# First and last weight matmul of every chunk carry one order mark: TensorE takes the 189 chunks whole, one behind the other

## Chip, cores and metric

One core of one Trainium2 chip runs the kernel. The metric is the device time of one execution in microseconds; lower is better. Every time in the text comes from the runs and the profiled execution of the kernel before.

## What is computed

Two transformer blocks, one behind the other, on a sequence of 256 positions with model width 1024, everything in float32. The first block has differential attention and block attention side by side; the second has two layers, each with retention, stick-breaking attention and a feed-forward part of width 4096.

```python
def first_block(x, p, ...):                       # DEPTH = 1
    h = rms_norm(x, norm_g[i])
    dq, dk, dv, dg, mq, mk, mv, mg, gates = split_in_proj(h @ w_in[i])
    y_a = (diff_attention(dq, dk, dv, ...) * silu(dg)) @ w_branch_diff[i]
    y_b = (moba_attention(mq, mk, mv) * silu(mg)) @ w_branch_moba[i]
    merged = sigmoid(g_a) * y_a + sigmoid(g_b) * y_b
    x = x + merged @ w_out[i]
    x = x + sigmoid(x @ w_ple_gate[i]) * (p[i] @ w_ple[i])
    return rms_norm(x, final_g)

def second_block(x, ...):
    for l in range(2):
        h = rmsnorm(x, g_mix[l])
        q_r, k_r, v_r, g_r, q_s, k_s, v_s, gate_a, gate_b = split(h @ w_in[l])
        ret = head_group_norm(retention(rotary(q_r), rotary(k_r), v_r)) * silu(g_r)
        sb = stick_breaking(q_s, k_s, v_s)
        merged = sigmoid(gate_a) * (ret @ p_ret[l]) + sigmoid(gate_b) * (sb @ p_sb[l])
        x = x + merged @ w_out[l]
        x = x + square(relu(rmsnorm(x, g_mlp[l]) @ w_up[l])) @ w_down[l]
    return rmsnorm(x, g_final)
```

## The kernel before

All weights come from DRAM as a stream of 189 chunks of 1 MB (`raw`, issued on SP's queue). This text numbers them C0 to C188 in stream order. Each chunk is split in two halves: ACT copies `raw` to a rounded high part `wh` (`split`, L294), DVE subtracts to get the low part `wl` (L295). The activations exist as the same kind of pair: `X2` is the normed input of a projection, hi by ACT (`norm_hilo`, L200) and lo by DVE (L201); `A2`, `B2` and `M2` are other such pairs (the names of the trace drop the digit). TensorE (PE) makes a product of full precision from three partial ones: `wh` against hi and lo together (one matmul of 512 columns) and `wl` against hi (256 columns), through the helper `mm` (L135).

The chunks that matter here: C0 to C36 are the first block (C20 is one of the four chunks `branch1` that multiply the attention's output `A2`; C33 to C36 are `w_ple_gate`). C37 to C112 are layer 0 of the second block: C37 is the first chunk of `w_in`, C38 and C39 the next ones; C66 is the first chunk of `p_sb`, which multiplies the stick-breaking output `B2`, eight heads that `sb_head` makes one after the other; C67 and C68 are gate chunks on `X2`; C77 to C80 are `w_out`, C81 to C88 the first of `w_up`. C113 to C188 are layer 1, where C142, C143, C144, C153 and C157 are what C66, C67, C68, C77 and C81 are in layer 0.

For a chunk with `fresh` set (C37, C77, C81, C113, C153, C157), `mm_t` first writes the partial products of the first six 128-row tiles of the input, and those of the last two tiles behind them, since the input is made tile by tile.

Of the attention, the last steps of a stick-breaking head are: `t` is exponentiated on ACT (L116), PE transposes it (L805, three matmuls), ACT and DVE split the result into `ph` and `pl` (L129, L130), PE multiplies it by the values (`mm3`, L138 to L140), and ACT and DVE split that into one tile of `B2`.

The order of the program is not the order of the source. The kernel is written with a tile framework whose scheduler simulates the engines and picks the next instruction of each engine among those that are free. An order token (`stamp_issue_order_token`) ties instructions with the same name to source order among themselves. Before the change the token "maps" stands on the last `mm` of the chunks i < LAST1 = 20 and on the score matmuls of the first block's attention heads (`soft_head`, L506). PE, ACT, DVE and POOL then execute their own queues in the order fixed by the scheduler, and wait on semaphores.

The main loop, at the end of `tile_blocks`, goes over the chunks: it issues the split of chunk i + 2 and the fetch of chunk i + 5, then runs `ch.banks(ch)` (the matmuls and what empties their banks), and lets each attention thread take one step.

Of the kernel before, what the change touches and what calls it, by code (L numbers as in the profile page):

```python
# [38 lines left out]
C_DEC = 1088  # L39
C_ALL = C_DEC + 4 * 384  # L40
NCHUNK = 189
LAST1 = 20


def _tables():
# [33 lines left out]
def tile_blocks(ctx: ExitStack, tc: tile.TileContext, a: dict, out: bass.AP):  # L79
    nc = tc.nc  # L80
    V, A, G, T = nc.vector, nc.scalar, nc.gpsimd, nc.tensor
# [21 lines left out]
    def acc():  # L103
        uid[0] += 1
        return psp.tile([P, 512], F32, tag="acc", bufs=NACC, name=f"acc_{uid[0]}")
# [23 lines left out]
        A.activation(hi, src, AF.Copy)  # L129
        V.tensor_sub(lo, src, f32(hi))  # L130

    last = [None]

    def mm(*args, **kw):
        last[0] = T.matmul(*args, **kw)  # L135

    def mm3(o, lh, ll, rh, rl, start, stop):
        T.matmul(o, lhsT=lh, rhs=rh, start=start, stop=False, skip_group_check=True)  # L138
        T.matmul(o, lhsT=lh, rhs=rl, start=False, stop=False, skip_group_check=True)  # L139
        T.matmul(o, lhsT=ll, rhs=rh, start=False, stop=stop, skip_group_check=True)  # L140


    xg = tl([GW + KT * S], "X")
# [33 lines left out]
    def use_consts():  # L177
        V.tensor_mul(gfm, g_fin, g_mix[0])
        V.tensor_scalar_mul(subg, subg, 1.0 - LAM_INIT)
        V.tensor_mul(lamv[:, 0:3:2], lamv[:, 0:3:2], lamv[:, 1:4:2])  # L180
        V.tensor_reduce(lam[:, 0:2], lamv[:, 0:3:2], AX.X, ALU.add)
        act(lam[:, 0:2], lam[:, 0:2], AF.Exp)
        V.tensor_sub(lam[:, 2:3], lam[:, 1:2], lam[:, 0:1])
        V.tensor_scalar_add(lam[:, 2:3], lam[:, 2:3], -LAM_INIT)
# [96 lines left out]
    def fetch(ch, n=1):  # L281

        ch.raw = shaped(ch, tl([2048], "raw", bufs=3))
        src = shaped(ch, a["wstream"][chunks.index(ch)])
        for k in pieces(ch, n):
            load(ch.raw[:, k], src[:, k])
            yield

    def split(ch, n=2):

        ch.wh = shaped(ch, tl([2048], "wh", F32R, bufs=3))
        ch.wl = shaped(ch, tl([2048], "wl", F32R, bufs=3))
        for k in pieces(ch, n):
            h = A.activation(ch.wh[:, k], ch.raw[:, k], AF.Copy)  # L294
            l = V.tensor_sub(ch.wl[:, k], ch.raw[:, k], f32(ch.wh[:, k]))  # L295
            yield h, l

    def mm_t(ch, ks, xs, j0, evac, n=2):
# [7 lines left out]
        def run(j, part, kinds):  # L306
            for m, i in ((m, i) for m in kinds for i in part):
                k, x = ks[i], xs[i]
                kw = dict(start=i == part[0] == 0 and m == kinds[0], stop=i == len(ks) - 1 and m == kinds[1],
                          skip_group_check=True)  # L310
                if m == 0:
                    mm(ps[j], lhsT=ch.wh[:, k, w[j]], rhs=x.rearrange("p c t -> p (c t)"), **kw)
                else:
                    mm(ps[j][:, 0:S], lhsT=ch.wl[:, k, w[j]], rhs=x[:, 0], **kw)
# [15 lines left out]
    def mm_2(ch, ks, xs, j0=0, n=2):  # L330

        ps = acc().rearrange("p (j t) -> p j t", j=2)
        for i, (k, x) in enumerate(zip(ks, xs)):
            for j in range(2):
                w = slice((j0 + j) * P, (j0 + j + 1) * P)
                mm3(ps[:, j], ch.wh[:, k, w], ch.wl[:, k, w], x[:, 0], x[:, 1], i == 0 and j == 0, i == len(ks) - 1)
        return ps

    def fold(ps, out=None):
# [6 lines left out]
    def mm_k(ch, ps, x, k0):  # L346

        for i in range(4):
            k = k0 + i
            for h in range(2):  # L350
                t = slice(h * P, (h + 1) * P)
                for n, (xs, ws) in enumerate(((x.h, ch.wh), (x.h, ch.wl), (x.l, ch.wh))):
                    mm(ps[h][0], lhsT=xs[:, k, t], rhs=ws[:, i], start=n == 0 and k == 0,
                       stop=n == 2 and k == KT - 1, skip_group_check=True)
# [26 lines left out]
    def chunk_2(w, c, x, evac, k0=0):  # L381
        def go(ch):
            ps = mm_2(ch, range(KT), [x().t[:, k] for k in range(KT)])
            run_pre()
            evac(ps, c)
        chunks.append(Chunk([wcols(w, c, k0)], go))
# [110 lines left out]
    def soft_head(idx, j, v, diff, wait):  # L497
# [42 lines left out]
        if diff:  # L540
            po = aux()[:, 0:S].rearrange("p (h e) -> p h e", h=2)
            h, l = wh[:, 0], wl[:, 0]
            vc = slice(j * P, (j + 1) * P)
            for i, (o, qt, kt) in enumerate(BLK):
                mm3(po[:, qt], h[:, o:o + P], l[:, o:o + P], vh[:, kt, vc], vl[:, kt, vc], i == 0, qt == kt)
            o = o_slot[idx % 2]
            ss = tl([2], "ss", bufs=2)
            for h in range(2):
                A.activation(o[:, h], po[:, h], AF.Square, accum_out=ss[:, h:h + 1])
            V.tensor_scalar(ss, ss, 1.0 / 128, EPS5, ALU.mult, ALU.add)  # L550
            G.tensor_tensor(ss, ss, mhalf[:, 0:2], ALU.pow)
            for h in range(2):
                A.activation(o[:, h], po[:, h], AF.Copy, scale=ss[:, h:h + 1])
            yield
            yield
            pt = aux()[:, 0:S]
            for h in range(2):
                T.transpose(pt[:, h * P:(h + 1) * P], o[:, h], ident)
            V.scalar_tensor_tensor(f, pt, subg, g1[:, idx], ALU.mult, ALU.mult)
        else:  # L560
            po = aux().rearrange("p (m q) -> p m q", m=2)
            vc = slice(j * P, (j + 1) * P)
            mm3(po, vh[:, 0, vc], vl[:, 0, vc], wh[:, :, 0:256], wl[:, :, 0:256], True, False)
            mm3(po[:, :, 128:256], vh[:, 1, vc], vl[:, 1, vc], wh[:, :, 256:384], wl[:, :, 256:384], False, True)
            for m in range(2):
                r = slice(m * 64, m * 64 + 64)
                V.tensor_mul(f[r], po[r, m], g1[r, idx])
# [78 lines left out]
    def branch1(c):  # L646
        def go(ch):
            if c == 0:
                start_merge()
            xs = [a1.t[:, k] for k in range(8)]  # L650
            ga, gb = sig(gates1, c, 0), sig(gates1, c, 1)
            pa, pb = mm_2(ch, range(4), xs[0:4]), mm_2(ch, range(4, 8), xs[4:8])
            V.tensor_mul(ga, ga, pa)
            V.tensor_mul(gb, gb, pb)
            G.tensor_add(ga, ga, gb)
            k = slice(2 * c, 2 * c + 2)
            hilo(mg.x.h[:, k], mg.x.l[:, k], ga)
            if c == 1:
                threads.append(ple_in())
        chunks.append(Chunk([wcols(("w_branch_diff", 0), c, 0, 4), wcols(("w_branch_moba", 0), c, 0, 4)], go))  # L660
# [21 lines left out]
    def ple(ch):  # L682
        for b in range(4):
            ps = mm_2(ch, range(2), [pt_.x.t[:, k] for k in range(2)], 2 * b)
            A.activation(pw[:, 2 * b:2 * b + 2], ps, AF.Copy)
# [352 lines left out]
    def drain(g):  # L1038
        for _ in g:
            pass  # L1040

    warm_up(WARM)
    f = fetch(chunks[0], 4)
# [7 lines left out]
    f = fetch(chunks[1], 2)  # L1051
# [5 lines left out]
    for i in range(2):  # L1057
        f = split(chunks[i], 4)
# [10 lines left out]
    for i, ch in enumerate(chunks):  # L1069
        if i + 2 < n:  # L1070
            drain(split(chunks[i + 2]))
        if i + 5 < n:
            drain(fetch(chunks[i + 5]))
        ready = list(threads)
        ch.banks(ch)
        if i < LAST1:
            tc.stamp_issue_order_token(last[0].ins, "maps")
        if i == 0:
            use_consts()
        for g in ready:  # L1080
            try:
                next(g)
            except StopIteration:
                threads.remove(g)
# [63 lines left out]
```

## Time and profile before

| what | value |
|---|---|
| median of 3 runs | 1146.5 us (1146.41 to 1147.41) |
| profiled execution | 1146.68 us, of which the span of the trace is 1144.8 us |
| PE busy | 1133.1 us, 6563 matmuls |
| DVE, ACT, POOL busy | 899.4, 708.4, 225.5 us |
| granted clock of TensorE, mean | 0.999 |

A busy share is an average over the span. PE has work nearly all the time, so the time is read from what PE does and from the few places where it waits. In the timeline a row gives the start of a run of like instructions and the time until the last of them ends; the next row may start before that, because matmuls overlap.

### The profile page before, as it was taken

Reading aid. Unit: us, or ns where it says so; the run is one execution under the profiler, and the core shown is the slowest. Engines: PE = TensorE matmul, PEld = TensorE weight load, DVE = VectorE, ACT = ScalarE, POOL = GpSimd, SP = SyncE. Lnnn points to the kernel's source line nnn. Section 1 sums busy time; section 2 is a strip of 40 time slices with the busy share of each in tenths; the row PEclk is TensorE's granted clock in tenths of the full one; section 3 lists DMA queues with packets and bytes.
Section 4 is the critical chain, followed back from the end, with each engine's and each line's share of the span. In section 5 each row is a group of like instructions: output and inputs, shape, how many; then the busy total and the mean of one; then the engine's idle time right before and its main releaser. Section 6 shows DMA issues by size and latency. Waiting matters only on the chain.

```text
span 1144.8 us, 17360 instructions
## 1 busy us (share of the span) xinstructions
PE 1133.1 (99%) x6563; PEld 994.1 (87%) x6563; DVE 899.4 (79%) x1487; ACT 708.4 (62%) x1286; POOL 225.5 (20%) x236
## 2 busy tenths in 40 slices
PE   9999999999999999999999999999999999999997
PEld 6888899998888888888888888888898888888887
DVE  6877787689988987788877778988886868967664
ACT  7788955476657665656654545556776656846542
POOL 0021231036442123220000014641121312000001
PEclk9999999999999999999999999999999999999999
DMA  8643455546544454545555556554444554555551
GB/s 319 230 162 132 148 184 185 184 175 206 195 175 163 147 182 149 204 181 202 185 184 187 197 188 210 182 191 163 182 148 147 201 193 177 207 198 184 185 184 38
DMA packets 32884, 207.63 MB, mean 181 GB/s; under 512 B 3873, under 2 KB 6433, under 8 KB 8737
## 3 DMA queue, kind: packets, MB, share of 16 engines
q1 hardware_dynamic: 32800, 206.52, 50.1%
q8 instruction: 52, 0.85, 0.3%
q14 instruction: 32, 0.25, 0.1%
HBM read 203.36 MB, written 1.05 MB: 179 GB/s over the span
## 4 chain that ended last, share of the span: by engine, by line
PE 93%; DVE 2%; DMA 1%; ACT 1%; issue 1%; POOL 1%; SPq 0%; POOLq 0%; DVEq 0%; ACTq 0%
PE acc L135 83%; PE acc L140 2%; PE acc L139 2%; PE acc L138 2%; PE aux L140 1%; PE aux L139 1%; PE aux L138 1%; DMA sig<-in_lambdas_dram 1%; PE aux L506 1%; DMA X<-in_xt_dram 1%; DVE wl L295 1%; PE aux L805 0%; ACT wh L294 0%; PE aux L489 0%; PE aux L535 0%
## 5 line engine op out<-in xcount | busy, mean ns | idle before, releaser
L295 DVE TENSOR_TENSOR wl<-raw,wh 128x1024 fp32r<-128x1024 f32 (+1 forms) x382 | 481.6, 1292 | 74.7 <-ACT wh L294 72.0
L294 ACT ACTIVATE wh<-raw 128x1024 fp32r<-128x1024 f32 (+1 forms) x382 | 380.8, 1044 | 144.3 <-PE acc L135 115.6
L135 PE MATMUL acc<-X,wh 128*128 128x512 f32 x1472 | 368.0, 393 | 0.3 <-DVE X L201 0.3
L135 PEld LDWEIGHTS acc<-X,wh 128*128 128x128 f32 x1472 | 266.8, 188 | 50.4 <-DVE X L201 0.5
L135 PE MATMUL acc<-X,wl 128*128 128x256 f32 x1472 | 202.3, 283 | 0.8 <-DVE f L343 0.8
L135 PEld LDWEIGHTS acc<-X,wl 128*128 128x128 f32 x1472 | 193.8, 191 | 9.6 <-DVE f L343 1.1
L342 ACT ACTIVATE f<-acc 128x256 f32<-128x256 f32 x216 | 80.1, 379 | 103.1 <-PE acc L135 102.2
L343 DVE TENSOR_TENSOR f<-f,acc 128x256 f32<-128x256 f32 x216 | 87.9, 415 | 67.8 <-ACT f L342 67.6
L135 PE MATMUL acc<-wh,X 128*128 128x512 f32 x448 | 119.0, 394 | 0.2
L135 PEld LDWEIGHTS acc<-wh,X 128*128 128x128 f32 x448 | 83.4, 188 | 18.3 <-ACT wh L294 1.5
L212 POOL TENSOR_TENSOR sq<-sq,f 128x256 f32<-128x256 f32 x24 | 26.5, 1102 | 263.6 <-ACT f L210 263.4
L624 POOL TENSOR_TENSOR sig<-f,nr 128x256 f32<-128x256 f32 x48 | 46.5, 976 | 119.9 <-DVE f L343 90.1
L693 DVE TENSOR_TENSOR X<-X,acc 128x256 f32<-128x256 f32 x112 | 45.9, 417 | 28.9 <-PE acc L135 27.8
L135 PE MATMUL acc<-wl,X 128*128 128x512 f32 x224 | 64.3, 394 | 0.0
L135 PE MATMUL acc<-B,wh 128*128 128x512 f32 x256 | 63.6, 391 | 0.0
L135 PE MATMUL acc<-A,wh 128*128 128x512 f32 x256 | 62.7, 391 | 0.0
L135 PEld LDWEIGHTS acc<-A,wh 128*128 128x128 f32 x256 | 47.0, 188 | 9.1
L135 PEld LDWEIGHTS acc<-B,wh 128*128 128x128 f32 x256 | 47.0, 188 | 9.0
L135 PEld LDWEIGHTS acc<-wl,X 128*128 128x128 f32 x224 | 41.7, 188 | 9.7 <-DVE wl L295 1.5
L135 PE MATMUL acc<-M,wh 128*128 128x512 f32 x192 | 48.0, 392 | 0.0
L573 POOL TENSOR_TENSOR G<-f,nr 128x256 f32<-128x256 f32 x24 | 21.5, 894 | 94.8 <-DVE f L343 94.7
L135 PEld LDWEIGHTS acc<-M,wh 128*128 128x128 f32 x192 | 34.6, 188 | 6.3
(229 smaller groups left out, 1623.4 us busy)
## 6 DMA issues: line engine op xcount, KB each, us to landing
raw<-in_wstream_dram SPq DMA_DIRECT2D x187, 1024.0 KB, 4.8
sig<-f SPq DMA_DIRECT2D x32, 64.0 KB, 4.4
B<-in_tables_dram SPq DMA_DIRECT2D x2, 768.0 KB, 5.9
raw<-in_wstream_dram SPq DMA_DIRECT2D x4, 256.0 KB, 4.4
raw<-in_wstream_dram SPq DMA_DIRECT2D x2, 512.0 KB, 7.4
M<-in_xn_dram SPq DMA_DIRECT2D x1, 1024.0 KB, 11.4
out_dram<-M SPq DMA_DIRECT2D x4, 256.0 KB, 2.2
X<-in_xt_dram SPq DMA_DIRECT2D x3, 256.0 KB, 6.1
```

The lines of the kernel that those rows point to most:

```text
L135: last[0] = T.matmul(*args, **kw)
L138: T.matmul(o, lhsT=lh, rhs=rh, start=start, stop=False, skip_group_check=True)
L139: T.matmul(o, lhsT=lh, rhs=rl, start=False, stop=False, skip_group_check=True)
L140: T.matmul(o, lhsT=ll, rhs=rh, start=False, stop=stop, skip_group_check=True)
L212: (V if k == KT - 1 else G).tensor_add(sq, sq, t)
L294: h = A.activation(ch.wh[:, k], ch.raw[:, k], AF.Copy)
L295: l = V.tensor_sub(ch.wl[:, k], ch.raw[:, k], f32(ch.wh[:, k]))
L342: A.activation(t, ps[:, S:2 * S], AF.Copy)
L343: V.tensor_add(t, t, ps[:, 0:S])
L573: G.tensor_mul(dst()[:, k], fold(ps), st.n.rb)
L624: G.tensor_mul(store[(c, i)][0][:, k % 2], fold(ps), st.n.rb)
L693: V.tensor_add(X[:, k], X[:, k], ps[:, o:o + S])
```

## The change

`mm` now collects every weight matmul of a chunk in `ends`, the projections made by `mm_2` (`mm3`) too. After `ch.banks(ch)` the first and the last of them get the token "maps", in all 189 chunks. No instruction is added or removed: both programs have 6563 matmuls. The line numbers of the changed kernel are 4 higher from the norm helpers on (L135 becomes L134, L138 to L140 become L142 to L144, L805 becomes L809).

```diff
-LAST1 = 20
...
-    last = [None]
+    ends = []
 
     def mm(*args, **kw):
-        last[0] = T.matmul(*args, **kw)
...
+        ends.append(T.matmul(*args, **kw))
+
+    def in_one(ends):
+
+        for ins in ends:
+            tc.stamp_issue_order_token(ins.ins, "maps")
+
+    def mm3(o, lh, ll, rh, rl, start, stop, f=T.matmul):
+        f(o, lhsT=lh, rhs=rh, start=start, stop=False, skip_group_check=True)
+        f(o, lhsT=lh, rhs=rl, start=False, stop=False, skip_group_check=True)
+        f(o, lhsT=ll, rhs=rh, start=False, stop=stop, skip_group_check=True)
...
-                mm3(ps[:, j], ch.wh[:, k, w], ch.wl[:, k, w], x[:, 0], x[:, 1], i == 0 and j == 0, i == len(ks) - 1)
+                mm3(ps[:, j], ch.wh[:, k, w], ch.wl[:, k, w], x[:, 0], x[:, 1], i == 0 and j == 0, i == len(ks) - 1, mm)
...
+        del ends[:]
         ch.banks(ch)
-        if i < LAST1:
-            tc.stamp_issue_order_token(last[0].ins, "maps")
+        in_one((ends[0], ends[-1]))
```

On PE the order changes at some fifteen places; written as rows of like instructions, PE's program has 2062 rows before and 1838 after. The two largest places follow.

PE at the start of layer 0, before: `wh_381` and `wl_382` are the weights of C37, `wh_390` and `wl_391` of C38, `wh_399` and `wl_400` of C39.

```order
L135 MATMUL acc_402_2680<-X2_366_2422,wh_381_2518 128x512 x2
L135 MATMUL acc_403_2693<-X2_366_2422,wl_382_2519 128x256 x3
L135 MATMUL acc_428_2790<-X2_366_2422,wh_390_2595 128x512 x2
L135 MATMUL acc_431_2818<-X2_366_2422,wl_391_2596 128x256
L135 MATMUL acc_403_2693<-X2_366_2422,wl_382_2519 128x256
L135 MATMUL acc_431_2818<-X2_366_2422,wl_391_2596 128x256 x3
L135 MATMUL acc_402_2680<-X2_366_2422,wh_381_2518 128x512
L135 MATMUL acc_428_2790<-X2_366_2422,wh_390_2595 128x512
L135 MATMUL acc_402_2680<-X2_366_2422,wh_381_2518 128x512
L135 MATMUL acc_428_2790<-X2_366_2422,wh_390_2595 128x512
L135 MATMUL acc_437_2854<-wh_399_2672,X2_366_2422 128x512 x4
L135 MATMUL acc_437_2854<-wl_400_2673,X2_366_2422 128x512 x4
```

The same place on PE after the change:

```order
L134 MATMUL acc_402_2680<-X2_366_2422,wh_381_2518 128x512 x2
L134 MATMUL acc_403_2693<-X2_366_2422,wl_382_2519 128x256 x4
L134 MATMUL acc_402_2680<-X2_366_2422,wh_381_2518 128x512 x2
L134 MATMUL acc_403_2693<-X2_366_2422,wl_382_2519 128x256
L134 MATMUL acc_402_2680<-X2_366_2422,wh_381_2518 128x512
L134 MATMUL acc_403_2693<-X2_366_2422,wl_382_2519 128x256
L134 MATMUL acc_403_2693<-X2_366_2422,wh_381_2518 128x512 x5
L134 MATMUL acc_402_2680<-X2_366_2422,wh_381_2518 128x512
L134 MATMUL acc_402_2680<-X2_366_2422,wl_382_2519 128x256 x6
L134 MATMUL acc_403_2693<-X2_366_2422,wh_381_2518 128x512
L134 MATMUL acc_403_2693<-X2_366_2422,wl_382_2519 128x256
L134 MATMUL acc_402_2680<-X2_366_2422,wh_381_2518 128x512
```

Before, matmuls of C38 and C39 stand between those of C37; after, all 32 matmuls of C37 stand ahead of the first of C38, and C39 stands behind C38. The order of ACT and DVE at this place is the same in both up to the last tile of `X2`.

PE at C66 of layer 0, before: `wh_705` and `wl_706` are C66, `wh_715` and `wl_716` C67, `wh_723` and `wl_724` C68, `aux_713` and `aux_714` the outputs of the last two heads.

```order
L135 MATMUL acc_726_4653<-B2_570_3677,wh_705_4523 128x512 x5
L135 MATMUL acc_728_4678<-B2_570_3677,wl_706_4524 128x256 x6
L135 MATMUL acc_733_4710<-X2_366_2422,wh_715_4592 128x512 x2
L135 MATMUL acc_726_4653<-B2_570_3677,wh_705_4523 128x512
L135 MATMUL acc_733_4710<-X2_366_2422,wh_715_4592 128x512 x6
L135 MATMUL acc_733_4710<-X2_366_2422,wl_716_4593 128x256 x2
L805 MATMUL aux_702_4515<-cst_2_62,t_679_4377 128x128 x3
L138 MATMUL aux_713_4574<-ph_700_4511,vh_637_4096 128x256
```

The same place on PE after the change:

```order
L134 MATMUL acc_726_4653<-B2_570_3677,wh_705_4523 128x512 x5
L134 MATMUL acc_728_4678<-B2_570_3677,wl_706_4524 128x256 x6
L134 MATMUL acc_726_4653<-B2_570_3677,wh_705_4523 128x512
L809 MATMUL aux_702_4515<-cst_2_62,t_679_4377 128x128 x3
L142 MATMUL aux_713_4574<-ph_700_4511,vh_637_4096 128x256
L143 MATMUL aux_713_4574<-pl_701_4512,vh_637_4096 128x256
L144 MATMUL aux_713_4574<-ph_700_4511,vl_638_4097 128x256
L142 MATMUL aux_713_4574<-ph_700_4511,vh_637_4096 128x128
L143 MATMUL aux_713_4574<-pl_701_4512,vh_637_4096 128x128
L144 MATMUL aux_713_4574<-ph_700_4511,vl_638_4097 128x128
L142 MATMUL aux_714_4583<-ph_703_4519,vh_637_4096 128x256
L134 MATMUL acc_728_4678<-B2_570_3677,wl_706_4524 128x256
```

Before, C67 begins after eleven matmuls of C66, and all of it and 11 matmuls of C68 stand ahead of the last head's first product (`aux_714`); after, that product follows the transposes and the other head (`aux_713`) directly, the rest of C66 stands behind it, and C67 begins only when C66 has ended.

## Rows read from the trace of the kernel before

**Rows 1.** The page: busy time of PE, and the chain that ended last, by line.
```profile
PE 1133.1 (99%) x6563; PEld 994.1 (87%) x6563; DVE 899.4 (79%) x1487; ACT 708.4 (62%) x1286; POOL 225.5 (20%) x236
...
PE acc L135 83%; PE acc L140 2%; PE acc L139 2%; PE acc L138 2%; PE aux L140 1%; PE aux L139 1%; PE aux L138 1%; DMA sig<-in_lambdas_dram 1%; PE aux L506 1%; DMA X<-in_xt_dram 1%; DVE wl L295 1%; PE aux L805 0%; ACT wh L294 0%; PE aux L489 
```

**Rows 2.** Waits of PE over the span: total us, times, longest.
```profile
PE aux L489 <- ACT sig L590: 1.3, 1, 1.3
PE aux L506 <- DVE ft L567: 0.8, 1, 0.8
...
PE aux L138 <- ACT M L129: 0.4, 1, 0.4
```

**Rows 3.** Timeline of PE, end of C144 (start us, us, operation, count).
```profile
888.66 2.08 PE L135 MATMUL acc<-X,wl 128*128 128x256 f32 x16
890.57 2.00 PE L135 MATMUL acc<-X,wh 128*128 128x512 f32 x8
892.41 0.84 PE L135 MATMUL acc<-A,wh 128*128 128x512 f32 x3
```

**Rows 4.** Timeline of PE, C37 to the start of C40.
```profile
242.09 0.63 PE L135 MATMUL acc<-X,wh 128*128 128x512 f32 x2
...
248.53 0.73 PE L135 MATMUL acc<-X,wh 128*128 128x512 f32 x2 [0.32 <-DVE X L201]
...
258.17 1.09 PE L135 MATMUL acc<-wh,X 128*128 128x512 f32 x4
259.10 1.07 PE L135 MATMUL acc<-wl,X 128*128 128x512 f32 x4
260.00 2.20 PE L135 MATMUL acc<-wh,X 128*128 128x512 f32 x9
```

**Rows 5.** Timeline of ACT, same place.
```profile
244.73 1.28 ACT L114 ACT_TABLE_LOAD   x1
246.03 0.51 ACT L200 ACTIVATE X<-X,gfm 128x256 fp32r<-128x256 f32 x1
```

**Rows 6.** Timeline of DVE, same place: the low parts of tiles 4 to 7.
```profile
247.52 3.60 DVE L201 SCALAR_TENSOR_TENSOR X<-X,gfm,X 128x256 fp32r<-128x256 f32 x4
```

**Rows 7.** Timeline of PE, C66 to the start of C69.
```profile
426.35 1.30 PE L135 MATMUL acc<-B,wh 128*128 128x512 f32 x5
...
442.89 1.22 PE L135 MATMUL acc<-X,wl 128*128 128x256 f32 x8 [0.77 <-DVE f L343]
...
445.80 1.52 PE L135 MATMUL acc<-A,wh 128*128 128x512 f32 x6
```

**Rows 8.** Timeline of ACT at C66.
```profile
427.05 1.28 ACT L114 ACT_TABLE_LOAD   x1
...
429.15 2.00 ACT L294 ACTIVATE wh<-raw 128x1024 fp32r<-128x1024 f32 x2
...
432.61 0.47 ACT L129 ACTIVATE ph<-aux 128x384 fp32r<-128x384 f32 x1
```

**Rows 9.** Timeline of DVE at C66.
```profile
433.11 0.56 DVE L130 TENSOR_TENSOR pl<-aux,ph 128x384 fp32r<-128x384 f32 x1 [0.37 <-ACT ph L129]
```

**Rows 10.** Timeline of PE at the end of C20: C21 begins.
```profile
150.81 2.00 PE L135 MATMUL acc<-X,wh 128*128 128x512 f32 x8
```

**Rows 11.** Timeline of DVE at the same place: last tile of the attention's output.
```profile
151.03 0.42 DVE L130 TENSOR_TENSOR A<-ft,A 128x256 fp32r<-128x256 f32 x1
```

**Rows 12.** Timeline of DVE at C142.
```profile
876.55 2.85 DVE L295 TENSOR_TENSOR wl<-raw,wh 128x1024 fp32r<-128x1024 f32 x2 [0.19 <-ACT wh L294]
```

**Rows 13.** Timeline of DVE at C81: split of a later chunk, last two low parts.
```profile
515.39 2.89 DVE L295 TENSOR_TENSOR wl<-raw,wh 128x1024 fp32r<-128x1024 f32 x2
518.21 0.87 DVE L201 SCALAR_TENSOR_TENSOR X<-X,X 128x256 fp32r<-128x256 f32 x2
```

**Rows 14.** Timeline of PE at the program's start.
```profile
1.30 4.21 PE L433 MATMUL aux<-one_r 128*128 128x512 f32 x9 [1.30 <-DVE one_r L164]
...
6.62 0.39 PE L135 MATMUL acc<-wl,X 128*128 128x512 f32 x1
```

**Rows 15.** Windows: PE, PEld, DVE, ACT, POOL busy (x), PEclk, DMA share, GB/s.
```profile
1138.00:1139.00 1.00, 0.31 (x3) 0.11 (x1) 0.97 (x5) 0.35 (x3) 0.00 (x0) 1.00 0.35 125
...
1143.30:1143.60 0.30, 0.00 (x0) 0.00 (x0) 0.00 (x0) 0.00 (x0) 0.00 (x0) 0.50 0.00 0
```

More of the change, by code (lines that the diff above doesn't have):

```diff
@@ L130, in hilo @@
         V.tensor_sub(lo, src, f32(hi))
-    last = [None]
+    ends = []
     def mm(*args, **kw):
-        last[0] = T.matmul(*args, **kw)
[L137 to L140, printed above, removed]
+        ends.append(T.matmul(*args, **kw))
[6 more added lines that the diff above has]
+        f(o, lhsT=ll, rhs=rh, start=False, stop=stop, skip_group_check=True)
     xg = tl([GW + KT * S], "X")
```

## The prediction

> **What bounds the kernel now.** I read the page first: PE is busy for 1133.1 of 1144.8 us, and 83% of the chain that ended last is one line of its matmuls [rows 1]. So the time is PE's own work plus its waits. The list of PE's waits is short; the largest entries are 1.3, 0.8 and 0.4 us [rows 2]. The reader is to see that the kernel before hides nearly every wait, and the question about the change is what it uses to hide them. I then looked at the timelines of PE, ACT and DVE at those places where the new order differs from the old, to see when the operands that PE will stand in front of are ready.
>
> **The price of the work itself.** Sixteen 256-column matmuls take 890.57 - 888.66 = 1.91 us and eight 512-column ones 892.41 - 890.57 = 1.84 us [rows 3], so 0.12 and 0.23 us each. A chunk of 16 + 16 is 3.68 + 1.91 = 5.59 us. No matmul is added or removed, so a term of the sum can only be a new wait, a wait that ends, or a change of a matmul's pace.
>
> **C37, the start of layer 0: +4.1 us.** Before, C37 starts at 242.09 and C40 at 260.00 + 4 x 0.23 = 260.9 [rows 4]; in these 18.8 us lie C37, C38 and C39 (5.6, 5.6 and 24 x 0.23 = 5.5), the norm's sums, a wait of 0.32 [rows 4] and some fourteen changes between shapes more than after, at 0.03 each (below) 0.4. After, C37 must go to its end before C38 begins. Eight of its matmuls, four of each kind, use tiles 0 to 3 and end at 242.09 + 4 x 0.23 + 4 x 0.12 = 243.5. The next wants the high part of tile 4. ACT makes it behind the split of a chunk, a sigmoid and a table load that lasts until 246.01, and it ends at 246.03 + 0.51 = 246.54 [rows 5]: PE is idle for 3.0 us. One matmul of 0.12 later it wants the low part of tile 4, which DVE begins at 247.52 [rows 6] and has at about 248.5, since that is where PE's wait for it ends before too [rows 4]: 1.8 us more. The other tiles follow every 0.9 us (four in 3.60) [rows 6], and PE's remaining 23 matmuls (12 x 0.23 + 11 x 0.12 = 4.1) keep pace. So C37 ends at about 252.7, and the whole stretch takes 18.8 - 0.3 - 0.4 + 4.8 = 22.9 us: C40 starts at 265.0 instead of 260.9. Nothing in front of these operands moves: ACT's and DVE's orders are the same here, and their chain starts from the end of C36, where both programs stand alike. What is queued behind the waiting matmul is all of PE, so the wait is paid in full unless a later wait shrinks.
>
> **C66 in layer 0: +3.3 us.** Before, C66 starts at 426.35 and C69 at 445.80 [rows 7]; in 19.45 us lie C66, C67, C68, the transposes and the last products of two heads, and a wait of 0.77 [rows 7]. After, PE does twelve matmuls of C66 (6 x 0.23 + 6 x 0.12 = 2.1), the three transposes and the first head's six products (together 0.9, nine at some 0.1), is through at 429.4, and wants `ph` of the last head. ACT loads a table from 427.05, then runs sigmoids and a split of 2.00, and starts `ph` at 432.61 [rows 8], which ends at 433.08: 3.7 us idle. The low part `pl` is there at 433.11 + 0.56 = 433.67 [rows 9]: 0.35 more. The last tile of `B2` has to pass from PE's product through ACT: 0.2 more. The old wait of 0.77 goes with its cause, a bank that was emptied late, and so do some six changes of shape, 0.2. So C69 starts 19.45 - 0.77 - 0.2 + 4.25 = 22.7 us after C66, at 449.1: +3.3. The cover that goes is C67 and C68.
>
> **Smaller places: +1.9 us.** C20's last six matmuls now come ahead of C21, at 150.81 [rows 10], but want a low part that DVE has at 151.45 [rows 11]: +0.55. C142 is what C66 is in layer 1, but there ACT is ahead of PE; what is left is that the last tiles of `B2` stand behind a split on DVE until 879.40 [rows 12]: +0.5. The first block's first attention head comes whole, ahead of work that filled its operands' delay; its wait of 0.8 [rows 2] can grow by as much or vanish; I take +0.4. At C81 and C157 the last low parts come behind a split at 518.21 [rows 13], and C82 and C83 hid that. In the new order of DVE one half of that split stands behind the first of them, and C77 frees DVE earlier, so I take 0.2 each (0 to 3 each, if DVE's backlog stays as it is). C33, C77, C113 and C153 have their last operands before PE gets to them: 0.
>
> **What comes back: -1.3 us.** Chunks that end earlier are evacuated earlier. The retention heads wait for products of this kind around 281 and 720 us (one of these waits is the 0.4 of [rows 2]); I take 0.5 each, and 0.3 for fewer changes between 256 and 512 columns. The four 512-column matmuls behind a change take 0.93 us, the next four 0.90 [rows 4], so a change costs 0.03.
>
> Together 4.1 + 3.3 + 1.9 - 1.3 = +8.0.
>
> **The clock: +1.7 us.** At the program's start nine matmuls of 512 columns take 4.21 us [rows 14], twice the later pace; full pace comes with the matmul at 6.62, 5.3 us after the first. [...] The wait of 1.3 us [rows 2] left it at 1.00. [...] If the clock falls there, PE works at half pace until it has been busy for a while: the bounds are 0 and half of 5.3 = 2.65 us; I take two thirds of the upper one, 1.7, since part of the low stretch lies in the wait itself. I forecast one such fall, at C37. [...]
>
> The sum is made against the profiled execution: 1146.7 + 8.0 + 1.7 = 1156.4 us. The 1.9 us between that time and its span stay as they are. That execution stands 0.2 above the median of 1146.5, so I say 1156.2. A change under 0.2%, 2.3 us, could not be told from none.
>
> **Rivals.**
> [...]
> - *It falls at both places.* 1146.5 + 8.0 + 2 x 1.7 = 1157.9, up to 1159.8 with 2.65 each. [...] For it: the wait at C66 is nearly as long as that at C37. Against: no row shows a fall after a wait of this length.
> - *DVE is late at C81 and C157.* If the low parts come at 519 as before, PE waits 1.5 at each place instead of 0.2, together +2.6 on the forecast: 1158.8. For it: DVE has hardly a gap there.
> - *The other side: not slower.* One mechanism could do it: fewer changes of what PE works on. The rows of PE's program fall by 224. If each break that goes were worth 10 / 224 = 0.045 us, all would be paid for and the time would be 1146.5; above that, faster. Against it: a change of shape costs 0.03 by [rows 4], and most of the 224 are changes of bank or chunk, at which the start times show nothing. At 0.03 for all 224 it would give back 6.7: 1149.5, still slower.
>
> **How the numbers follow.** Forecast (all waits, one fall of the clock) 0.45; clock stays 0.30; two falls 0.12; DVE late 0.06; not slower 0.07. The range from 1151.5 to 1159.5 holds the first four with the errors of their waits and leaves out the last and the ends of the second and third, about 0.15. Faster by over 0.2%: 0.03; within 0.2%: 0.05; slower: 0.92.
>
> **What would show it.** In the profile after, PE should wait for `X2` at C37 some 3.0 us (ACT) and 1.8 (DVE), and for `ph` at C66 some 3.7 (ACT). C40 should start about 4 us later than before, C69 another 3 later. In the windows after each wait the granted clock tells whether it fell; a fall with PE's matmuls at twice their start-to-start time is the 1.7. The prediction is wrong if those waits are short because ACT reaches the operands sooner than before, or if PE's busy time without waits is clearly smaller.

## The result, and the profile after

The change takes 1158.55 us (median of 4 runs, 1157.46 to 1159.25) against 1146.48 of the kernel before: ratio 1.0103, 95% interval [1.0091, 1.0115]. A second set of runs gave 1158.47 (1157.98 to 1159.25) and 1.0105 [1.0090, 1.0120]. It is slower by 12 us.

The list of PE's waits after the change (us in total, times, longest):

```profile
PE aux L142 <- ACT ph L128: 3.6, 1, 3.6
PE acc L134 <- ACT X L204: 2.9, 1, 2.9
PE acc L134 <- DVE X L205: 1.5, 1, 1.5
...
PE aux L493 <- ACT sig L594: 1.1, 1, 1.1
PE aux L510 <- DVE ft L571: 0.8, 1, 0.8
```

Three entries are larger than any entry of [rows 2]: the high part of `X2` at C37 and `ph` at C66, which are new, and the low part of `X2` at C37, for which PE waited 0.32 before. The timeline of PE at C37, which answers to [rows 4]:

```profile
242.42 0.63 PE L134 MATMUL acc<-X,wh 128*128 128x512 f32 x2
...
246.91 0.44 PE L134 MATMUL acc<-X,wl 128*128 128x256 f32 x1 [2.94 <-ACT X L204]
248.84 0.80 PE L134 MATMUL acc<-X,wh 128*128 128x512 f32 x1 [1.49 <-DVE X L205]
...
249.64 2.77 PE L134 MATMUL acc<-X,wh 128*128 128x512 f32 x6
252.21 1.48 PE L134 MATMUL acc<-X,wl 128*128 128x256 f32 x6
...
266.82 1.98 PE L134 MATMUL acc<-wh,X 128*128 128x512 f32 x8
```

The reader is to see two things. The waits are there, in the order and with the releasers of the prediction. Behind them the matmuls are slow: six of 512 columns take 252.21 - 249.64 = 2.57 us, 0.43 each instead of 0.23. C40 starts at 266.82 + 4 x 0.23 = 267.7. Windows over the two places show the clock (PE, PEld, DVE, ACT, POOL busy, then the granted clock):

```profile
240.00:247.00 7.00, 4.06 (x31) 3.54 (x29) 7.00 (x8) 5.91 (x10) 3.65 (x4) 1.00 0.43 152
247.10:249.00 1.90, 0.41 (x2) 0.16 (x1) 1.87 (x4) 1.90 (x7) 1.35 (x2) 0.50 0.71 181
249.00:253.90 4.90, 4.90 (x15) 4.16 (x16) 4.13 (x7) 2.63 (x8) 3.68 (x5) 0.50 0.74 306
253.95:256.00 2.05, 2.05 (x12) 1.77 (x11) 0.50 (x2) 0.65 (x3) 0.00 (x0) 1.00 0.00 0
430.00:438.20 8.20, 5.90 (x38) 5.15 (x36) 4.87 (x10) 5.86 (x10) 1.46 (x2) 1.00 0.35 128
438.30:440.00 1.70, 0.53 (x2) 0.53 (x2) 1.32 (x3) 1.39 (x4) 0.00 (x0) 0.50 0.00 0
440.00:445.00 5.00, 5.00 (x16) 3.94 (x16) 0.77 (x3) 0.38 (x1) 0.00 (x0) 0.50 0.58 210
445.10:447.00 1.90, 1.90 (x13) 1.72 (x13) 0.00 (x0) 0.45 (x2) 0.00 (x0) 1.00 0.00 0
```

The granted clock falls to 0.50 at both places, at C66 between 438.2 and 438.3, while PE waits until 439.47, and at C37 by 247.1, just behind the end of the first of two waits at 246.91; it is back at 1.00 in the windows from 253.95 and from 445.10. In the two low windows of each place PE is busy for 0.41 + 4.90 = 5.3 and 0.53 + 5.00 = 5.5 us. At C66 the timelines of PE and ACT, which answer to [rows 7, 8]:

```profile
432.70 1.30 PE L134 MATMUL acc<-B,wh 128*128 128x512 f32 x5
...
439.47 0.58 PE L142 MATMUL aux<-ph,vh 128*128 128x256 f32 x1 [3.58 <-ACT ph L128]
...
457.74 1.98 PE L134 MATMUL acc<-A,wh 128*128 128x512 f32 x8
```

```profile
435.49 1.99 ACT L298 ACTIVATE wh<-raw 128x1024 fp32r<-128x1024 f32 x2
437.39 1.66 ACT L115 ACTIVATE sig<-sig 128x512 f32<-128x512 f32 x3
438.95 0.47 ACT L128 ACTIVATE ph<-aux 128x384 fp32r<-128x384 f32 x1
```

C66 to C69 now takes 457.74 - 432.70 = 25.0 us, where it took 19.45. Where the 12 us of the profiled execution went is read from the start of the first matmul of a chunk in both traces, stretch by stretch:

| stretch | before, us | change, us | difference |
|---|---|---|---|
| start to C7 | 51.49 | 51.10 | -0.4 |
| C20 to C22 | 12.37 | 13.03 | +0.66 |
| C37 to C40 | 18.81 | 25.31 | +6.50 |
| C40 to C46 | 38.07 | 37.56 | -0.51 |
| C66 to C69 | 19.45 | 25.04 | +5.59 |
| C69 to C113 (C81 in it) | 245.26 | 245.49 | +0.23 |
| C113 to C126 | 81.18 | 80.51 | -0.67 |
| C142 to C145 | 18.14 | 18.67 | +0.53 |
| C145 to the last matmul (C157 in it) | 245.62 | 245.88 | +0.26 |

Everything between these stretches is equal within 0.05 us. The sum is 12.2.

### The profile page after: what moved, and what is told of

The parts are those of the page before. It is cut to its first block, busy times and chain, and to the rows that moved or that the text cites. A ratio compares the mean times of both kernels' runs of the same rounds, so it can differ in the third digit from the quotient of the medians.

```text
span 1157.2 us, 17329 instructions
## 1 busy us (share of the span) xinstructions
PE 1138.3 (98%) x6563; PEld 997.9 (86%) x6563; DVE 895.9 (77%) x1487; ACT 711.5 (61%) x1286; POOL 213.8 (18%) x236
## 4 chain that ended last, share of the span: by engine, by line
PE 94%; DVE 2%; DMA 1%; ACT 1%; issue 0%; SPq 0%; POOLq 0%; POOL 0%; DVEq 0%
PE acc L134 88%; PE aux L143 1%; PE aux L144 1%; PE aux L142 1%; DMA sig<-in_lambdas_dram 1%; PE aux L510 1%; DVE wl L299 1%; DMA X<-in_xt_dram 1%; PE aux L809 0%; ACT wh L298 0%; PE aux L493 0%; PE aux L539 0%; PE aux L780 0%; SPq L125 0%; ACT sig L115 0%
## 5 line engine op out<-in xcount | busy, mean ns | idle before, releaser
L299 DVE TENSOR_TENSOR wl<-raw,wh 128x1024 fp32r<-128x1024 f32 (+1 forms) x382 | 474.8, 1274 | 72.0 <-ACT wh L298 69.5
L134 PE MATMUL acc<-X,wh 128*128 128x512 f32 x1472 | 369.2, 394 | 1.5 <-DVE X L205 1.5
L134 PEld LDWEIGHTS acc<-X,wh 128*128 128x128 f32 x1472 | 268.4, 189 | 53.1 <-DVE X L205 2.3
L134 PEld LDWEIGHTS acc<-X,wl 128*128 128x128 f32 x1472 | 193.0, 192 | 11.2 <-ACT X L204 3.4
L134 PE MATMUL acc<-X,wl 128*128 128x256 f32 x1472 | 199.3, 284 | 2.9 <-ACT X L204 2.9
L134 PE MATMUL acc<-wh,X 128*128 128x512 f32 x448 | 118.2, 393 | 0.6 <-ACT wh L298 0.6
L134 PE MATMUL acc<-A,wh 128*128 128x256 f32 (+1 forms) x512 | 109.4, 337 | 0.4 <-DVE A L129 0.4
L134 PEld LDWEIGHTS acc<-wh,X 128*128 128x128 f32 x448 | 83.2, 188 | 18.5 <-ACT wh L298 1.6
L134 PEld LDWEIGHTS acc<-A,wh 128*128 128x128 f32 x512 | 87.3, 190 | 10.0 <-DVE A L129 0.6
L216 POOL TENSOR_TENSOR sq<-sq,f 128x256 f32<-128x256 f32 x24 | 22.3, 927 | 266.6 <-ACT f L214 266.6
L134 PE MATMUL acc<-A,wl 128*128 128x256 f32 x384 | 70.4, 283 | 0.0
L134 PE MATMUL acc<-B,wh 128*128 128x512 f32 x256 | 65.0, 398 | 0.0
L628 POOL TENSOR_TENSOR sig<-f,nr 128x256 f32<-128x256 f32 x48 | 40.1, 837 | 130.1 <-DVE f L347 127.2
L134 PE MATMUL acc<-wl,X 128*128 128x512 f32 x224 | 63.6, 393 | 0.0
L134 PEld LDWEIGHTS acc<-A,wl 128*128 128x128 f32 x384 | 57.6, 191 | 1.3
L134 PEld LDWEIGHTS acc<-B,wh 128*128 128x128 f32 x256 | 48.2, 193 | 9.3
L134 PEld LDWEIGHTS acc<-wl,X 128*128 128x128 f32 x224 | 41.6, 188 | 9.8 <-DVE wl L299 1.5
L134 PE MATMUL acc<-M,wh 128*128 128x512 f32 x192 | 47.2, 391 | 0.0
```

The lines of the kernel that those rows point to most:

```text
L134: ends.append(T.matmul(*args, **kw))
L216: (V if k == KT - 1 else G).tensor_add(sq, sq, t)
L628: G.tensor_mul(store[(c, i)][0][:, k % 2], fold(ps), st.n.rb)
```

## The experiments

My theory after the result: the loss is the two waits, which the chunks behind C37 and C66 filled before, and a fall of the clock in each; the rest of the change adds up to less than 1.5 us. The rivals: the loss is spread over the new order, or the waits only bring forward what PE would have waited for later.

**The mark left off C38 and C39.**

```diff
-        in_one((ends[0], ends[-1]))
+        if i not in (38, 39):
+            in_one((ends[0], ends[-1]))
```

> The change with the mark left off C38 and C39 alone, so that both may again fill C37's wait. My theory (the time went into two waits of TensorE and the clock that falls in each): the wait for X2 at C37 and the fall of the clock there go, about 4.1 + 2.4 = 6.5 us, so 1152 us; the wait for ph at C66 (3.6) and its fall stay. Rival (the waits at C37 only bring forward what PE would wait for later, and the loss is spread over the new order): less than 3 us comes back, 1156 or more.

Measured: 1153.19 us (1152.32 to 1154.44), ratio 1.0059 [1.0044, 1.0074]. C37 to C40 takes 18.82 us, as before; C66 to C69 25.01, as with the change. The granted clock is 1.00 at C37:

```profile
240.00:256.00 16.00, 15.69 (x90) 13.29 (x89) 13.33 (x17) 10.79 (x24) 8.74 (x10) 1.00 0.47 182
```

So 5.4 us of the medians, and 6.5 of the stretch, go with these two marks. A part of that had been made good behind it: C40 to C46 takes 38.36 us here and 37.56 with the change. So 0.8 us of the rival that the waits only bring forward a later wait may be right.

**The mark left off C67 and C68.** The same edit with `(67, 68)`.

> The change with the mark left off C67 and C68 alone, so that both may again fill C66's wait. My theory: the wait for ph (3.6) and the fall of the clock at C66 go, about 3.3 + 2.4 = 5.7 us, so 1153 us; C37 keeps its waits and its fall. Rival (spread over the new order): less than 3 us comes back, 1156 or more.

Measured: 1153.63 us (1153.12 to 1154.94), ratio 1.0060 [1.0043, 1.0077]. C66 to C69 takes 19.44 us, C37 to C40 25.53. Each of the two stretches keeps its time when the other is freed. Of what is earned at C66 nothing is taken back behind it: C69 to the last matmul takes the same as with the change, within 0.1 us.

**The mark left off all four.** The same edit with `(38, 39, 67, 68)`.

> The mark left off C38, C39, C67 and C68; all other 185 chunks keep both marks. My theory: the two places are all of the loss, the rest of the change adds up to nothing: 1146.5 us within 1. Rival (the rest of the order costs too, at C20, C81, C157 and C142): 1148.5 or more. Rival of the other sign (fewer breaks between chunks are worth something): 1145 or less.

Measured: 1147.76 us (1147.43 to 1148.76), ratio 1.0011 [1.0001, 1.0020], with a mean granted clock of 0.998 or 0.999 in all ten runs. The two places are 11 of the 12 us. One us is left: 1147.76 lies 0.3 us beyond the 1146.5 within 1 that I had given for nothing, so the rival that the smaller places cost too is right in kind, below its 1148.5.

**Idle matmuls in the waits.** The change with twelve matmuls of 512 columns (ones times ones, into a bank that nobody reads) added behind the first matmul of C37 and of C66.

```diff
...
     def mm(*args, **kw):
+        if fill[0] and len(ends) == 1:
+            ps = acc()
+            in_one([T.matmul(ps, lhsT=one_r, rhs=one_r[:, None, :].to_broadcast([P, 4, P]), start=True, stop=True)
+                    for _ in range(fill[0])])
         ends.append(T.matmul(*args, **kw))
...
+        fill[0] = FILL.get(i, 0)
```

> The change as it is, with twelve idle matmuls of 512 columns (ones times ones, into a bank that nobody reads) behind the first matmul of C37 and of C66: PE has 2.7 us of work more where it waits anyway, so the waits keep their end. If the fall of the clock is caused by the idle time and costs 2.4 us at each place: the granted clock stays at 1.00 through both places and the time is 1158.5 - 4.8 = 1153.7 us. If the clock falls in spite of them (too short a filling, or the wait of 1.8 us at C37 suffices): 1156 to 1158.5. If the fillings themselves are late work on PE: above 1158.5.

Measured: 1156.33 us (1155.31 to 1156.86), ratio 1.0084 [1.0069, 1.0099]; all its runs have a mean clock of 0.998. Its windows over the two places:

```profile
247.00:256.00 9.00, 7.28 (x39) 5.89 (x38) 7.81 (x14) 6.85 (x18) 5.07 (x6) 1.00 0.57 205
430.00:438.00 8.00, 7.20 (x40) 6.07 (x38) 4.30 (x7) 6.74 (x11) 1.47 (x2) 1.00 0.31 123
438.00:447.00 9.00, 8.81 (x52) 7.54 (x53) 4.75 (x11) 4.04 (x9) 0.00 (x0) 1.00 0.34 118
```

PE does more work and the program ends sooner: in this trace the clock stays at 1.00. C37 to C40 takes 23.01 us and C66 to C69 23.04. Against the kernel before that is +4.20 and +3.59: the price of the waits alone. Against the change it is -2.30 and -2.00: the price of the two falls in its profiled execution. The gain of the medians is smaller, 2.2 where I expected 4.8; by the time alone, 1156.33 lies where I had expected it if the clock fell in spite of the filling.

**The change and the filled version once more, side by side.** The change has an unused constant more.

> The change again, with an unused constant more, beside the filled version on one chip, for the spread. If the falls of the clock are what differs from run to run: the mean granted clock of its runs varies between about 0.992 and 0.997, and the time goes with it, from 1159.5 down to about 1156; median 1158. If the spread has another cause: times without relation to the clock.

> The filled version again (twelve idle matmuls of 512 columns behind the first matmul of C37 and of C66). If the falls are what it removes: all runs at a clock of 0.998, spread under 2 us, median 1156, and the difference to the change of the same call is what the falls cost per run on the average: 2 to 4 us, for falls of about 1 to 2 us each.

Measured: the change 1158.47 us (1157.98 to 1159.25), the filled version 1157.39 (1154.74 to 1158.62). This expectation failed for the filled version: its profiled execution has a mean clock of 0.998 and takes 1154.74, but of the others two have a mean clock of 0.997 and 0.996 and take 1157.24 and 1158.62. Whether the waits that the filling leaves (1.5 us for `X2`, 0.8 for `ph`) let the clock fall in these two is not shown, since they have no trace; the mean alone does not tell it, for one run with only the last matmuls marked has 0.997 at 1146.91 us.

The change now has a second trace, with falls at both places again, and the one at C66 is shorter. Its windows at C37 and at C66:

```profile
245.90:252.70 6.80, 4.55 (x12) 3.59 (x13) 6.14 (x8) 4.85 (x13) 5.06 (x6) 0.50 0.74 267
440.50:443.80 3.30, 3.11 (x9) 2.50 (x9) 0.42 (x1) 0.17 (x1) 0.00 (x0) 0.50 0.66 278
443.90:446.00 2.10, 2.10 (x14) 1.87 (x14) 0.14 (x1) 0.62 (x3) 0.00 (x0) 1.00 0.00 0
```

C37 to C40 takes 24.81 us in it and C66 to C69 24.48, so here the falls cost 1.80 and 1.44 us against the 23.01 and 23.04 of the filled version. Time and mean clock of the runs of these kernels go together, though not fully:

| kernel | time (mean granted clock) |
|---|---|
| change | 1157.46 (0.996), 1157.98 (0.995), 1158.06 (0.995), 1158.36 (0.996), 1158.58 (0.995), 1159.05 (0.993), 1159.25 (0.993), 1159.25 (0.993) |
| filled | 1154.74 (0.998), 1155.31 (0.998), 1155.86 (0.998), 1156.80 (0.998), 1156.86 (0.998), 1157.24 (0.997), 1157.54 (0.998), 1158.62 (0.996) |

The filled version's 1154.74 and 1157.54 at the same 0.998 show that something else varies by up to 3 us. A part of it is the start of the program: in the ten traces with the change's order up to there, C7 begins between 51.0 and 52.2 us. The two traces of the filled version differ by 0.8 us up to C7 and by less than 0.1 behind it. The two of the change differ by 0.1 up to C7 and by 1.1 in the two stretches with the low clock. The rest stays open, since the other executions have no trace.

**`X2` ahead of the split.** The change, with the split of C39 ordered behind the parts of `X2` on ACT and on DVE (`in_order` stamps one token on each of the two engines).

```diff
-        norm_hilo(n, X[:, k], k)
+        pair = norm_hilo(n, X[:, k], k)
+        if n is nxt.n:
+            in_order(pair)
...
-            drain(split(chunks[i + 2]))
+            for pair in split(chunks[i + 2]):
+                if i == 37:
+                    in_order(pair)
```

> The change, with the split of C39 put behind the high and low parts of X2's tiles on ACT and DVE (order marks on both engines), so that tile 4 of X2 comes sooner: its high part some 2 us and its low part some 2.5 us earlier. My theory: the waits of PE at C37 shrink from 2.9 + 1.5 to about 1.2 + 0.8, and with so little idle time the clock stays at 1.00 there: 1158.5 - 2.4 - 2.1 = 1154 us; C66 keeps its wait and its fall. If the clock falls there all the same: 1156. If the split that now comes later makes C39 wait, or the norm's chain behind it the retention heads: the gain goes back in part, and a new wait stands in PE's list.

Measured: 1155.25 us (1153.97 to 1155.85), ratio 1.0071 [1.0057, 1.0084]. The waits shrink as expected; the clock falls in spite of that. PE and windows at C37:

```profile
243.62 0.62 PE L134 MATMUL acc<-X,wh 128*128 128x512 f32 x2
245.37 0.38 PE L134 MATMUL acc<-X,wl 128*128 128x256 f32 x1 [1.12 <-ACT X L204]
246.37 0.80 PE L134 MATMUL acc<-X,wh 128*128 128x512 f32 x1 [0.62 <-DVE X L205]
```

```profile
243.00:246.30 3.30, 1.63 (x9) 0.95 (x7) 3.27 (x5) 3.27 (x6) 1.24 (x3) 1.00 0.59 218
246.40:249.70 3.30, 3.30 (x8) 2.68 (x9) 2.27 (x4) 3.30 (x9) 3.30 (x5) 0.50 0.60 220
249.80:252.00 2.20, 2.20 (x16) 2.01 (x15) 2.20 (x2) 1.44 (x3) 2.11 (x2) 1.00 0.00 0
```

The clock is 1.00 up to 246.3 and 0.50 from 246.4, behind idle times of 1.12 and 0.62 us with one matmul between them. My theory that so little idleness keeps the clock up did not hold. The low stretch is shorter here, 3.4 us instead of 6.8. That it is so because the waits are shorter is not shown: the mean clock of this execution is 0.996, against 0.993 with two stretches of 6.8 us, so by an estimate from these means the one at C66 is some 2.5 to 5 us here, behind a wait of 3.6 us that nothing was done about.

**`ph` ahead of the split.** The change, with the split of C68 ordered behind the last head's `ph` on ACT.

```diff
-        A.activation(hi, src, AF.Copy)
-        V.tensor_sub(lo, src, f32(hi))
+        h = A.activation(hi, src, AF.Copy)
+        return h, V.tensor_sub(lo, src, f32(hi))
...
-        hilo(h_, l_, pt[:, 0:384])
+        pair = hilo(h_, l_, pt[:, 0:384])
+        if h == 7:
+            in_order(pair)
...
-            drain(split(chunks[i + 2]))
+            for pair in split(chunks[i + 2]):
+                if i == 66:
+                    in_order(pair)
```

> The change, with the split of C68 (2.0 us of ACT) put behind the last head's ph on ACT; nothing else moves but ph's place on ACT and DVE. My theory: PE's wait at C66 is ACT's queue ahead of ph, so it shrinks from 3.6 to 1.6 us. The clock: since it fell for 3.4 us even at 1.1 + 0.6 us of idleness, it may fall here for as long: 1158.5 - 2.0 - 0.7 = 1155.8 us; if it stays at 1.00 there: 1158.5 - 4.0 = 1154.5. Rival (ph waits for PE's transposes or for the head's chain on DVE, not for the split): no change of the wait, 1158.

Measured: 1157.88 us (1155.07 to 1159.32), ratio 1.0088 [1.0072, 1.0103]. The wait for `ph` shrinks from 3.6 to 1.7 us, so it was ACT's queue. The time hardly follows. PE and windows at C66:

```profile
438.32 0.39 PE L142 MATMUL aux<-ph,vh 128*128 128x256 f32 x1 [1.69 <-ACT ph L128]
...
440.49 0.85 PE L134 MATMUL acc<-B,wl 128*128 128x256 f32 x2 [0.48 <-ACT B L128]
441.14 4.05 PE L134 MATMUL acc<-B,wh 128*128 128x512 f32 x9
```

```profile
436.00:439.20 3.20, 1.30 (x9) 0.96 (x9) 0.98 (x2) 3.20 (x8) 1.46 (x2) 1.00 0.00 0
439.30:446.00 6.70, 6.22 (x20) 5.17 (x20) 2.98 (x4) 1.41 (x3) 0.00 (x0) 0.50 0.42 157
446.10:448.00 1.90, 1.90 (x11) 1.62 (x11) 0.91 (x3) 1.40 (x3) 0.00 (x0) 1.00 0.00 0
```

The clock falls when the wait is over, between 439.2 and 439.3 where the wait ends at 438.32, and nearly the whole low stretch is work, 6.22 of 6.70 us: C66 to C69 takes 24.38 us, only 0.66 less than in the first trace of the change and 0.10 less than in the second. As an estimate: without a fall it would take the filled version's 23.04 less the 1.9 us of the shorter wait, and up to 0.7 more for the two small waits that are new, so the fall costs some 2.5 to 3.2 us here. In this execution most of the shorter wait was paid back by a dearer fall; that this is so in every execution is not shown. The four executions range from 1155.07 (mean clock 0.997) to 1159.32 (0.992).

**One mark in place of two.** Only the last matmul of every chunk marked, and only the first.

```diff
-        in_one((ends[0], ends[-1]))
+        in_one((ends[-1],))
```

> Only the last weight matmul of each of the 189 chunks carries the mark (the first none), so a chunk may begin inside the one ahead of it. My theory: it is the pair, last of one chunk ahead of first of the next, that forbids the filling; the last mark alone leaves C38, C39, C67 and C68 free to fill: 1146.5 to 1147 us, no wait at C37 or C66, clock at 1.00. Rival (any order mark over all chunks costs, since the scheduler is bound): above 1149.

```diff
-        in_one((ends[0], ends[-1]))
+        in_one(ends[:1])
```

> Only the first weight matmul of each chunk carries the mark, in all 189. My theory: as with the last mark alone, the chunks behind C37 and C66 may still fill their waits: no wait of more than 1 us there, clock at 1.00, 1146 to 1148 us. Rival (the order of the first matmuls is what keeps PE from filling): above 1152.

Measured: last only 1146.70 us (1146.35 to 1147.34), ratio 0.9999 [0.9990, 1.0008]; first only 1146.47 (1145.80 to 1146.83), 0.9995 [0.9986, 1.0004]. Either mark alone is free: the stretches at C37 (18.83 and 18.84 us) and C66 (19.33 and 19.45) are those of before. It is the pair, the last of one chunk ahead of the first of the next, that forbids the filling.

**The smaller places.** The marks left off every chunk that filled a wait.

```diff
-        in_one((ends[0], ends[-1]))
+        if i not in (21, 38, 39, 67, 68, 82, 83, 143, 144, 158, 159):
+            in_one((ends[0], ends[-1]))
```

> The marks left off all chunks that filled a wait: C21, C38, C39, C67, C68, C82, C83, C143, C144, C158 and C159. By the starts of the chunks the places C20 (0.35), C81 (0.25), C142 (0.55) and C157 (0.25) cost 1.4 us together, which is the 1.0 that was left with C37 and C66 free, and the 0.7 gained at C118 stays: 1146.3 us, 0.5 under the kernel before. Rival (what was left is spread, or is the start of the program): 1147.5 as with C37 and C66 free.

Measured: 1146.14 us (1145.68 to 1146.50), ratio 0.9995 [0.9986, 1.0004]. The stretches at C20 (12.37), C142 (18.14) and C69 to C113 (245.26) are those of before, and C113 to C126 keeps its 80.51. So the us that was left is C20, C81, C142 and C157. C40 to C46 takes 38.34, 0.27 more than before. As a time of the whole, the version can't be told from the kernel before.

**The gain alone.** The kernel before, with both marks on C113 to C129 only.

```diff
-        in_one((ends[0], ends[-1]))
+        if 113 <= i < 130:
+            in_one((ends[0], ends[-1]))
+        elif i < 20:
+            in_one(ends[-1:])
```

> The kernel before with both marks on C113 to C129 alone (the start of layer 1, where the changed kernel gains 0.7 us on the one before by the starts of its chunks). If that gain belongs to these marks: 1146.0, 0.6 under the kernel before. If it was only earned by the waits ahead of it: 1146.7, no change.

Measured: 1146.09 us (1145.80 to 1146.84), ratio 0.9993 [0.9984, 1.0002]. C113 to C126 takes 80.51 us instead of 81.18, so the gain of 0.67 belongs to these marks and needs no wait ahead of it. As a time of the whole it can't be told from no change.

## Why the prediction was right, and where a size was off

Direction and range held: 1158.55 lies between 1151.5 and 1159.5, slower by 12 us where 9.7 was forecast. Point by point:

- **C37, +4.1.** Measured 4.20 without the fall of the clock. The two waits were forecast as 3.0 (ACT) and 1.8 (DVE) and are 2.94 and 1.49; the releasers are the forecast ones.
- **C66, +3.3.** Measured 3.59 without the fall; the wait for `ph` was forecast as 3.7 and is 3.58. That the split of 2.0 us stands ahead of it on ACT was shown by moving it.
- **Smaller places, +1.9.** C20 +0.66 (forecast 0.55), C142 +0.53 (0.5), C81 and C157 some 0.25 each (0.2). The 0.4 that I gave to the first head is nothing: its wait is 0.78 us at 123.58 before and 0.79 at 123.24 with the change, and C7 to C20, where it lies, takes 93.26 and 93.31. The start of the program came out 0.4 shorter in the profiled execution, but it varies by 1.2 us between executions. The rival with DVE late at C81 and C157 is ruled out by the 0.25.
- **What comes back, -1.3.** C40 to C46 gives -0.51 and C113 to C126 -0.67. The cause that I gave, earlier evacuation of chunks that end earlier, fits the second: the marks there suffice, and the wait of 0.37 us at 721 is gone. For the first it is not what the runs show: with C38 and C39 free and all other marks there, the stretch takes 38.36, longer than the 38.07 before, and only where C37 waits is the wait of 0.21 us, at 281.75 before, gone and the time between 37.5 and 37.6. Whether the delay at C37 does this or the order that goes with it stays open. That number was right by luck.
- **The clock, +1.7.** This is the term that was mis-sized, and by the number of falls. The step that failed is "I forecast one such fall, at C37". In both traces of the change there are two: 2.30 and 2.00 us in the first, 1.80 and 1.44 in the second, 4.3 and 3.2 us together. The 1.7 itself was my estimate from the pace at the program's start [rows 14], where the granted clock reads 1.00, and no run shows it; it lies among these four prices. Its reason, that part of the low stretch lies in the wait itself, fits too: of 6.8 us PE was busy 5.3 and 5.5 in the first trace, and 4.6 at C37 in the second, so a fifth to a third was waiting. The rival with two falls named the place, with a chance of 0.12 and 1157.9 us. By the number alone the rival with DVE late, 1158.8, lies nearer, but its waits are not there. The windows above show 0.50 at both places, where the waits are for ACT and DVE.
- **Why one fall was too few.** My reason against a fall at C66 was that no row shows one after a wait of this length. The rows of the kernel before could not show it, since their longest wait is 1.3 us. The runs with shorter waits had a fall too: behind 1.12 and 0.62 us at C37, and behind 1.69 and 0.21 at C66.
- **A reading that was wrong.** The rival on the other side counted 224 rows that PE's program loses. About 130 of them are no fewer breaks: where the product of three stood in two or three rows of different lines, it is now recorded from one line, so equal neighbours fall into one row. With lines left out the rows fall by 90 only. The rival was even weaker than I made it, and the whole order with the places of the waits freed gained 0.3 us by the start of its last matmul.

That the lost cover was C38, C39, C67 and C68 is shown by leaving the marks off them. That the loss is not spread is shown by the equal stretches between.

## What to carry to other kernels

Where a scheduler lets a later block fill the wait of an earlier one, read for each such place when the late operand comes, and add the waits up before the blocks are put in strict order: the sum of such places was right to 0.6 us here, in the two traces of the filled version, though two of its smaller terms were wrong in cause or in size. To each such wait add the price of a possible fall of TensorE's clock, 1.3 to 2.5 us in the traces here, and expect the time to vary between executions: the eight of the change lie between 1157.46 and 1159.25 us. A shorter wait need not help in full: where the wait for `ph` was cut from 3.6 to 1.7 us, the clock fell all the same, and the median went down by 0.6 to 0.7.

## What the runs showed of the hardware that was not expected

In the version with `X2` ahead of the split the granted clock fell from 1.00 to 0.50 at 246.4 us, after idle times of only 1.12 and 0.62 us with one matmul between them. A wait of 1.55 us for `X2` left it at 1.00 in the filled version (the window from 247 to 256 us), and the profiled execution with all places freed, where PE waits 1.7 us for `sig`, has a mean of 0.999. How long it stays low at one place differs between executions: at C66, behind a wait of 3.6 us in both, some 6.8 us in one trace of the change and some 3.3 in the other. The change's mean clock was 0.993 in three of eight runs and 0.995 or 0.996 in the others. In the windows above a low stretch lasted some 3.3 us (C66 in the second trace of the change, C37 with `X2` ahead of the split) or some 6.8 (the others). By the stretches from chunk to chunk, against those of the filled version, a fall cost 1.3 us (C66 in the version with `X2` ahead of the split, 24.34 against 23.04) to 2.5 us (C37 with C67 and C68 free, 25.53 against 23.01). At the program's start full pace came 5.3 us after the first matmul in the kernel before [rows 14], and 5.6 us after it in the first trace of the change (the matmul at 6.86, behind one at 1.30), with the granted clock at 1.00 there in both. Adding 24 useless matmuls, 5.5 us of work, inside the waits made the program shorter by 1.1 to 2.2 us by the medians.
